# Half of the up product's k-tiles by seven block products, and the feed-forward in three parts

## The chip, the cores and the metric

The kernel runs on one NeuronCore of a Trainium2 chip. The metric is the device time of one execution in microseconds (us). Three runs of the kernel before took 1993.22, 1993.96 and 1994.38 us; their median, 1993.96 us, is the time before.

## The reference, cut to what matters

The reference is one layer of an encoder block on 256 tokens of width 2048: gated token mixers, cross-attention to 256 memory tokens, and a feed-forward. The change touches the feed-forward alone, in float32 throughout:

```
def _swiglu(h, w_gu, w_down):
    g, u = jnp.split(h @ w_gu, 2, axis=-1)     # h: 256 x 2048, w_gu: 2048 x 11264
    return (jax.nn.silu(g) * u) @ w_down       # w_down: 5632 x 2048
...
x = x + _swiglu(_rms(x, norm_ffn[i]), w_gu[i], w_down[i])
```

The first half of `w_gu` is called gate, the second half up, and `w_down` down.

## The kernel before, in words

**A product.** The large products go through `gemm_i` (lines 124 to 161). One call makes 512 output columns for all 256 tokens. The inner width is cut into k-tiles of 128; the tokens into two halves of 128, each with an accumulator in PSUM of 512 columns (a bank). Float32 accuracy is had from two rounded parts of each operand: with h and l for the high and low part, a product of one k-tile and one half of the tokens is three matmuls, h by h, h by l and l by h (lines 150 to 152), each with 128 columns of activations loaded as the stationary operand and 512 columns of weights streaming past. So 16 k-tiles are 16 x 2 x 3 = 96 matmuls.

**The weights.** `load_w` brings four k-tiles (1 MB, 2048 columns) into one of two buffers named `raw`, on SyncE's queue (SP). `split_w` (lines 110 to 122) makes from two k-tiles, 1024 columns, the high part on ScalarE (ACT, line 120) and then the low part, weights less high part, on VectorE (DVE, line 121). Both go into a tile named `wsp`, of which there are four. ACT may write a `wsp` only when the last matmul on the split of four before is done.

**The feed-forward** (lines 1048 to 1075). The normalised input lies transposed in `x2T_h` and `x2T_l`, 16 k-tiles each. A loop of 11 rounds makes 512 columns a round: a gate product (16 k-tiles), evacuated by ACT with SiLU to two tiles `gt`; an up product (16 k-tiles), evacuated by DVE, which multiplies it by `gt`; and `to_operand`, eight transposes on TensorE (PE, line 859) and two splits into `hT_h` and `hT_l`. The transposes of a round stand among the matmuls of the next gate. After the 11 rounds, four down products run over all 44 k-tiles of `hT`, and DVE adds the residual `x1` and the sums go out. Ahead of the feed-forward stands the output product of the cross-attention (`w_xo`, line 1038), whose four blocks are added to `x1` and turned by `to_operand` into `x2T`.

**The order.** A scheduler lays down each engine's order when the program is built; on the chip each engine follows its own order and waits on semaphores. Loads and splits of weights have the highest priority there (`WPRI`), evacuations the second (`EPRI`).

## Time and profile before

| | |
|---|---|
| median of three runs | 1993.96 us |
| the profiled execution's own time | 1992.28 us |
| its span, first to last instruction | 1990.5 us |
| PE busy | 1979.3 us, 99% |
| DVE busy | 1248.9 us, 63% |
| ACT busy | 973.9 us, 49% |
| DMA | 377.78 MB, 190 GB/s mean |
| gate and up, 11 rounds | 1256 to 1745 us of the span |
| down, four products | 1745 us to the end |

The profile is of one execution. Busy times count instructions under way; matmuls overlap each other, so that one shows as 0.39 us where the next starts 0.227 us later. What a matmul costs in a dense stream is therefore read from starts, not from durations; the same holds, less strongly, for DVE. "Idle before" and its releaser tell whom an engine waited for.

### The profile page before, as it was taken

The page shows a single profiled execution, that of the slowest core. Times are in us where ns is not written, and L with a number is a line of the kernel's source. Part 1 is how long each engine was busy: PE and PEld are TensorE (multiplying, and loading weights), DVE is VectorE, ACT ScalarE, POOL GpSimd, SP SyncE. Part 2 cuts the span into 40 slices and gives each one's busy share as a digit, 9 for nine tenths or more (in the row PEclk, how much of TensorE's full clock was granted, in tenths as well). Part 3 has the DMA queues.
Part 4 walks back from the last instruction along what each step waited for, and adds up shares of the span by engine and source line. Part 5 has one row for each costly group of instructions (what it writes and reads, how often), then busy time and mean ns, then how long its engine had stood idle before and what let it go on. Part 6 is the DMA issues. An engine that isn't in the chain of part 4 may idle for free.

```text
span 1990.5 us, 25137 instructions
## 1 busy us (share of the span) xinstructions
PE 1979.3 (99%) x9880; PEld 1665.5 (84%) x9880; DVE 1248.9 (63%) x1804; ACT 973.9 (49%) x1332; POOL 79.4 (4%) x142
## 2 busy tenths in 40 slices
PE   9999999999999999999999999999999999999999
PEld 7998888887888888888888888888888888888887
DVE  8968886769987967655545655545544444444443
ACT  7555655555444354554544545444444444443332
POOL 1002202000000000011000100000000000000000
PEclk9999999999999999999999999999999999999999
DMA  8554455455555655765455444555555555555553
GB/s 315 187 175 159 136 190 202 161 197 179 183 189 187 204 189 210 276 212 190 169 193 187 148 149 169 190 190 190 190 190 191 190 190 190 191 190 201 201 202 136
DMA packets 60406, 377.78 MB, mean 190 GB/s; under 512 B 6912, under 2 KB 8064, under 8 KB 18816
## 3 DMA queue, kind: packets, MB, share of 16 engines
q1 hardware_dynamic: 56880, 367.42, 52.6%
q0 software_dynamic: 2112, 6.82, 1.5%
q10 hardware_dynamic: 1296, 1.95, 0.3%
q8 instruction: 77, 1.26, 0.2%
q14 instruction: 41, 0.34, 0.0%
HBM read 374.06 MB, written 2.10 MB: 189 GB/s over the span
## 4 chain that ended last, share of the span: by engine, by line
PE 94%; DVE 2%; DMA 1%; ACT 1%; issue 1%; POOL 1%; SPq 0%; DVEq 0%; ACTq 0%; POOLq 0%
PE acc L151 28%; PE acc L150 28%; PE acc L152 28%; PE acc L175 2%; PE acc L176 2%; PE acc L177 2%; PE sm L859 1%; DMA raw<-in_w_in_dram 1%; DVE wsp L121 1%; PE sm L419 1%; PE sm L1028 1%; PE sm L1002 1%; ACT wsp L120 0%; PE sm L943 0%; PE sm L223 0%
## 5 line engine op out<-in xcount | busy, mean ns | idle before, releaser
L121 DVE TENSOR_TENSOR wsp<-raw,wsp 128x1024 fp32r<-128x1024 f32 (+2 forms) x700 | 833.2, 1193 | 648.1 <-ACT wsp L120 645.3
L120 ACT CAST wsp<-raw 128x1024 fp32r<-128x1024 f32 (+2 forms) x700 | 715.3, 1029 | 862.2 <-PE acc L152 638.9
L150 PE MATMUL acc<-wsp,x2T_h 128*128 128x512 f32 x704 | 274.9, 391 | 0.0
L151 PE MATMUL acc<-wsp,x2T_h 128*128 128x512 f32 x704 | 274.9, 391 | 0.0
L152 PE MATMUL acc<-wsp,x2T_l 128*128 128x512 f32 x704 | 273.9, 389 | 0.0
L151 PE MATMUL acc<-wsp,xT_h 128*128 128x512 f32 (+2 forms) x704 | 262.6, 374 | 1.3 <-DVE wsp L121 1.2
L152 PE MATMUL acc<-wsp,xT_l 128*128 128x512 f32 (+2 forms) x704 | 260.8, 371 | 0.0
L150 PE MATMUL acc<-wsp,xT_h 128*128 128x512 f32 (+2 forms) x704 | 260.1, 373 | 0.3 <-ACT wsp L120 0.3
L151 PEld LDWEIGHTS acc<-wsp,xT_h 128*128 128x128 f32 x704 | 132.2, 188 | 27.1 <-DVE wsp L121 3.4
L152 PEld LDWEIGHTS acc<-wsp,x2T_l 128*128 128x128 f32 x704 | 132.2, 188 | 27.1
L150 PEld LDWEIGHTS acc<-wsp,x2T_h 128*128 128x128 f32 x704 | 132.2, 188 | 27.1
L151 PEld LDWEIGHTS acc<-wsp,x2T_h 128*128 128x128 f32 x704 | 132.2, 188 | 27.0
L150 PEld LDWEIGHTS acc<-wsp,xT_h 128*128 128x128 f32 x704 | 132.0, 188 | 24.4 <-issue 1.3
L152 PEld LDWEIGHTS acc<-wsp,xT_l 128*128 128x128 f32 x704 | 132.3, 188 | 23.1 <-issue 0.3
L150 PE MATMUL acc<-wsp,hT_h 128*128 128x512 f32 x352 | 137.0, 389 | 0.0
L151 PE MATMUL acc<-wsp,hT_h 128*128 128x512 f32 x352 | 137.0, 389 | 0.0
L152 PE MATMUL acc<-wsp,hT_l 128*128 128x512 f32 x352 | 136.9, 389 | 0.0
L152 PE MATMUL acc<-wsp,eT_l 128*128 128x512 f32 x256 | 100.1, 391 | 0.0
L151 PE MATMUL acc<-wsp,eT_h 128*128 128x512 f32 x256 | 100.0, 390 | 0.0
L150 PE MATMUL acc<-wsp,eT_h 128*128 128x512 f32 x256 | 99.8, 390 | 0.0
L175 PE MATMUL acc<-xT_h,wsp 128*128 128x256 f32 x352 | 99.3, 282 | 0.0
L176 PE MATMUL acc<-xT_l,wsp 128*128 128x256 f32 x352 | 99.2, 282 | 0.0
(376 smaller groups left out, 2828.3 us busy)
## 6 DMA issues: line engine op xcount, KB each, us to landing
raw<-in_w_gu_dram SPq DMA_DIRECT2D x88, 1024.0 KB, 4.7
raw<-in_w_in_dram SPq DMA_DIRECT2D x68, 1024.0 KB, 4.9
raw<-in_w_down_dram SPq DMA_DIRECT2D x44, 1024.0 KB, 4.7
raw<-in_w_xkv_dram SPq DMA_DIRECT2D x32, 1024.0 KB, 4.7
raw<-in_w_ii_dram SPq DMA_DIRECT2D x22, 1024.0 KB, 4.9
raw<-in_w_out_dram SPq DMA_DIRECT2D x16, 1024.0 KB, 5.3
raw<-in_w_xq_dram SPq DMA_DIRECT2D x16, 1024.0 KB, 4.7
raw<-in_w_xo_dram SPq DMA_DIRECT2D x16, 1024.0 KB, 4.7
```

Of the source, the lines that this page charges most:

```text
L120: S.copy(hi[:, :n], raw[:, c0:c1])
L121: V.tensor_tensor(lo[:, :n], raw[:, c0:c1], hi[:, :n].bitcast(F32), ALU.subtract)
L150: PE.matmul(o, sh, h, start=(kt == 0), stop=False)
L151: PE.matmul(o, sh, lw, start=False, stop=False)
L152: mm = PE.matmul(o, xl[:, kt, t * P:(t + 1) * P], h, start=False, stop=(kt == nk - 1))
L175: PE.matmul(po, h, xh[:, kt, :], start=(kt == 0), stop=False)
L176: PE.matmul(po, h, xl[:, kt, :], start=False, stop=False)
L177: mm = PE.matmul(po, lo[:, j * P:(j + 1) * P], xh[:, kt, :], start=False, stop=(kt == nk - 1))
L419: PE.matmul(pb[e][:, i * T:(i + 1) * T], bT[q:q + 32, i, c, :], u[q:q + 32, c, :], start=True, stop=True, tile_position=(q, 0))
L859: PE.transpose(px[:, j * T + t * P:j * T + (t + 1) * P], srcs[t][:, (kp + j) * P:(kp + j + 1) * P], ident)
L1002: PE.matmul(pS[:, t * T:(t + 1) * T], qx[:, qi, d, t * P:(t + 1) * P], kx[:, ki, d], start=(d + i == 0), stop=(d == 3 and i == 2))
L1028: PE.matmul(po[:, j * T:(j + 1) * T], vx[:, vi, m, c0:c0 + P], pT[pi][:, m * T:(m + 1) * T], start=(m + i == 0), stop=(m == 1 and i == 2))
```

## The change

**Seven products for eight.** In the up product, k-tiles 0 to 7 stay as they were. K-tiles 8 to 15 are taken as four pairs of k-tiles (2, "q"), two halves of the tokens and two halves of the 512 columns ("h"): a 2 x 2 block product. Strassen's scheme in Winograd's form makes it from seven products of blocks where the plain form has eight. A product is now four pairs by three matmuls, each 128 columns stationary and 256 streaming (lines 232 to 234). Three of the seven run on in half banks of the two accumulators, on top of what k-tiles 0 to 7 left there; four go to banks of their own.

**Sums of the activations.** `pairs_operand` makes, for the blocks of k-tiles 8 to 15, the four sums and differences S1 to S4 beside the blocks themselves, and splits all eight; they lie in the upper half of `x2T_h` and `x2T_l` and in new tiles `x2S_h` and `x2S_l`. It replaces `to_operand` for two of the four blocks of `w_xo`.

**Sums of the weights.** `seven_weights` loads the last 8 k-tiles of an up (two loads of 1 MB) into a tile `sraw`, of which there is one, in the middle of the gate's loads, and makes four sums of 1024 columns on DVE (lines 192 to 195), one in place in `sraw` and three in a tile `ts`, of which there is one. Each of the seven weight blocks is then split as before (lines 224 and 225), 1024 columns at a time.

**Sums of the products.** ACT copies two of the products from PSUM to tiles `u` (line 240); DVE makes eight additions of 256 columns (line 251), six of which write to PSUM in place.

**Three parts.** The 11 rounds are cut into 4, 4 and 3. After each part, the four down products run over that part's 16, 16 or 12 k-tiles; the first two parts add to `x1` in place, the third adds and writes out. `hT` is a tile for one part.

The diff, cut to its core:

```diff
-    def gemm_i(xh, xl, nk, src, off, n, evac, first=None, e=0):
+    def gemm_i(xh, xl, nk, src, off, n, evac, first=None, e=0, then=None):
...
                 raw = load_w(blk, kk * n)
+                if k == 4 and then is not None:
+                    then()
...
+    def seven_weights(src, off):
+        raw = spool[0].tile([P, NS * 512], F32, tag="sraw", name=nm("sraw"))
+        off += P * (KD - NS) * 512
+        for i in range(2):
+            load_w(src[off:off + P * 2048].rearrange("(p f) -> p f", p=P), 2048,
+                   raw[:, i * 2048:(i + 1) * 2048])
+            off += P * 2048
+        ts = spool[0].tile([P, 3, 4, 256], F32, tag="ts", name=nm("ts"))
+        b11, b12, b21, b22 = blocks(raw)
+        t1, t2, t4 = (ts[:, i] for i in range(3))
+        V.tensor_tensor(t1, b11, b12, ALU.add)
+        V.tensor_tensor(b12, b12, b22, ALU.add)
+        V.tensor_tensor(t2, t1, b22, ALU.add)
+        V.tensor_tensor(t4, t2, b21, ALU.add)
+        return raw, ts
...
+    def gemm_s(xh, xl, sop, src, off, evac, weights):
...
+        def parts(b):
+            t = wp.tile([P, 2112], F32R, tag="wsp", name=nm("wsp"), bufs=4)
+            hi, lo = (t[:, 1024 * i + 48:1024 * i + 1072].rearrange("p (i c) -> p i c", c=256)
+                      for i in range(2))
+            with tc.high_priority(offset=WPRI):
+                S.copy(hi, b)
+                V.tensor_tensor(lo, b, hi.bitcast(F32), ALU.subtract)
+            return hi, lo
+
+        def product(o, i, b, start, stop):
+            hi, lo = parts(b)
+            for p in range(4):
+                sh, sl = sop(0, p, i), sop(1, p, i)
+                PE.matmul(o, sh, hi[:, p], start=start and p == 0, stop=False)
+                PE.matmul(o, sh, lo[:, p], start=False, stop=False)
+                PE.matmul(o, sl, hi[:, p], start=False, stop=stop and p == 3)
+            return o
...
+        product(c(0, 0), A12, b21, False, False)
+        product(c(0, 1), S4, b22, False, True)
+        u1 = kept(side(A11, b11))
+        v(c(0, 0), c(0, 0), u1, ALU.add)
+        u5 = kept(side(S1, t1))
+        p6 = side(S2, t2)
+        v(u1, p6, u1, ALU.add)
+        v(c(0, 1), c(0, 1), u5, ALU.add)
+        v(c(0, 1), c(0, 1), u1, ALU.subtract)
+        evac(0, pp[0])
+        product(c(1, 0), A22, t4, False, True)
+        p7 = side(S3, t3)
+        v(c(1, 1), c(1, 1), u5, ALU.add)
+        v(u1, p7, u1, ALU.add)
+        v(c(1, 0), c(1, 0), u1, ALU.add)
+        v(c(1, 1), c(1, 1), u1, ALU.subtract)
+        evac(1, pp[1])
...
+            V.tensor_tensor(b[:, S1], b[:, A21], b[:, A22], ALU.subtract)
+            V.tensor_tensor(b[:, S3], b[:, A11], b[:, A21], ALU.subtract)
+            V.tensor_tensor(b[:, S2], b[:, S1], b[:, A11], ALU.subtract)
+            V.tensor_tensor(b[:, S4], b[:, S2], b[:, A12], ALU.add)
...
-    hTh = p3.tile([P, KF, T], F32R, name="hT_h")
+    for c0, c1 in FF_PARTS:
+        nk = 4 * (c1 - c0)
+        hTh = p3.tile([P, nk, T], F32R, tag="hh", name=nm("hT_h"))
...
-        off = gemm_i(gTh, gTl, KD, a["w_gu"], off, 512, evg)
-        off = gemm_i(gTh, gTl, KD, a["w_gu"], off, 512, evu)
-        to_operand(sg, hTh, hTl, 4 * n)
+            def then(up=up, o=off + CH):
+                up["w"] = seven_weights(a["w_gu"], o)
+            off = gemm_i(mixed(0), mixed(1), KD, a["w_gu"], off, 512, evg, then=then)
+            off = gemm_s(gT[0], gT[1], sop, a["w_gu"], off, evu, up["w"])
+            to_operand(sg, hTh, hTl, 4 * (n - c0))
...
+                    if not last:
+                        d = x1[:, t, n * 512:(n + 1) * 512]
+                        V.tensor_tensor(d, po, d, ALU.add)
+                        return
```

**PE, from k-tile 13 on in the up of the second round.** `acc` is an accumulator, `wsp` a split of the weights, `x2T` and `x2S` the activations and their sums. Before:

```order
L150 MATMUL acc_11223<-wsp_11322,x2T_h 128x512
L151 MATMUL acc_11223<-wsp_11322,x2T_h 128x512
L152 MATMUL acc_11223<-wsp_11322,x2T_l 128x512
L150 MATMUL acc_11222<-wsp_11337,x2T_h 128x512 [waits Activation_49]
L151 MATMUL acc_11222<-wsp_11337,x2T_h 128x512 [waits DVE_49]
L152 MATMUL acc_11222<-wsp_11337,x2T_l 128x512
```

Now, where the whole k-tiles end and the first of the seven products begins:

```order
L211 MATMUL acc_11321<-wsp_11371,x2T_h 128x512
L212 MATMUL acc_11321<-wsp_11371,x2T_h 128x512
L213 MATMUL acc_11321<-wsp_11371,x2T_l 128x512
L232 MATMUL acc_11320<-wsp_11386,x2T_h 128x256 [waits Activation_49]
L233 MATMUL acc_11320<-wsp_11386,x2T_h 128x256 [waits DVE_49]
L234 MATMUL acc_11320<-wsp_11386,x2T_l 128x256
```

The matmuls of k-tiles 8 to 15 now have 256 columns instead of 512; there are 84 of them a round for the 48 of before, and a new split is taken up every 12, as before.

**DVE, from the end of an up to the next gate.** `wsp<-raw` is a low part, `gt<-acc` the evacuation of the up, `hT_l` the low part of the next operand. Before:

```order
L121 TENSOR_TENSOR wsp_11322<-raw_11320,wsp_11322 128x1024 [waits DMAHW5_49,Activation_49]
L121 TENSOR_TENSOR wsp_11337<-raw_11320,wsp_11337 128x1024 [waits Activation_49]
L121 TENSOR_TENSOR wsp_11374<-raw_11372,wsp_11374 128x1024 [waits DMAHW6_49,Activation_49]
L121 TENSOR_TENSOR wsp_11389<-raw_11372,wsp_11389 128x1024 [waits Activation_49]
L121 TENSOR_TENSOR wsp_11406<-raw_11404,wsp_11406 128x1024 [waits DMAHW7_49,Activation_49]
L1060 SCALAR_TENSOR_TENSOR gt_11088<-acc_11222,rst,gt_11088 128x512 [waits PE_49]
L1060 SCALAR_TENSOR_TENSOR gt_11089<-acc_11223,rst,gt_11089 128x512 [waits PE_49]
L121 TENSOR_TENSOR wsp_11421<-raw_11404,wsp_11421 128x1024 [waits Activation_49]
L121 TENSOR_TENSOR wsp_11438<-raw_11436,wsp_11438 128x1024 [waits DMAHW0_49,Activation_49]
L215 TENSOR_TENSOR hT_l<-sm_11354,hT_h 128x512 [waits Activation_49]
L215 TENSOR_TENSOR hT_l<-sm_11361,hT_h 128x512 [waits Activation_49]
```

Now, from the last two of the seven low parts on; `u` are the copies that ACT made, `sm` a product in a bank of its own:

```order
L225 TENSOR_TENSOR wsp_11473<-ts_11219,wsp_11473 128x1024 [waits Activation_49]
L225 TENSOR_TENSOR wsp_11489<-sraw_11216,wsp_11489 128x1024 [waits Activation_49]
L251 TENSOR_TENSOR acc_11320<-acc_11320,u_11432 128x256 [waits Activation_49]
L121 TENSOR_TENSOR wsp_11529<-raw_11527,wsp_11529 128x1024 [waits DMAHW6_49,Activation_49]
L251 TENSOR_TENSOR u_11432<-sm_11453,u_11432 128x256 [waits DVE_49,PE_49]
L251 TENSOR_TENSOR acc_11320<-acc_11320,u_11451 128x256 [waits Activation_49]
L121 TENSOR_TENSOR wsp_11544<-raw_11527,wsp_11544 128x1024 [waits Activation_49]
L251 TENSOR_TENSOR acc_11321<-acc_11321,u_11451 128x256 [waits PE_49]
L251 TENSOR_TENSOR acc_11320<-acc_11320,u_11432 128x256 [waits DVE_49]
L121 TENSOR_TENSOR wsp_11569<-raw_11559,wsp_11569 128x1024 [waits DMAHW7_49,Activation_49]
L121 TENSOR_TENSOR wsp_11584<-raw_11559,wsp_11584 128x1024 [waits Activation_49]
```

and, following on without a gap, through the weight sums (`ts`, `sraw`) of the next round to the gate's sixth split:

```order
L1214 SCALAR_TENSOR_TENSOR gt_11178<-acc_11320,rst,gt_11178 128x512 [waits DVE_49]
L251 TENSOR_TENSOR u_11432<-sm_11488,u_11432 128x256
L192 TENSOR_TENSOR ts_11564<-sraw_11561 128x1024 [waits DMAHW1_49,DMAHW0_49]
L251 TENSOR_TENSOR acc_11321<-acc_11321,u_11432 128x256 [waits DVE_49]
L193 TENSOR_TENSOR sraw_11561<-sraw_11561 128x4x256 [waits DVE_49]
L194 TENSOR_TENSOR ts_11564<-ts_11564,sraw_11561 128x1024
L251 TENSOR_TENSOR acc_11321<-acc_11321,u_11432 128x256 [waits DVE_49]
L195 TENSOR_TENSOR ts_11564<-ts_11564,sraw_11561 128x1024 [waits DVE_49]
L121 TENSOR_TENSOR wsp_11601<-raw_11599,wsp_11601 128x1024 [waits DMAHW2_49,Activation_49]
L1214 SCALAR_TENSOR_TENSOR gt_11179<-acc_11321,rst,gt_11179 128x512 [waits DVE_49]
L121 TENSOR_TENSOR wsp_11616<-raw_11599,wsp_11616 128x1024 [waits Activation_49]
```

Between the last split of the up and the fifth of the next gate there now stand eight additions and four weight sums. The first sum waits for the loads of `sraw`, and every later low part stands behind it in DVE's order.

**SP's queue, loads of weights at the start of the third round's gate.** Before:

```order
L102 DMA raw_11288<-in_w_gu_dram 128x2048 [waits DMAHW2_49,DVE_49]
L102 DMA raw_11320<-in_w_gu_dram 128x2048 [waits DMAHW3_49,DVE_49]
L102 DMA raw_11372<-in_w_gu_dram 128x2048 [waits DMAHW4_49,DVE_49]
L102 DMA raw_11404<-in_w_gu_dram 128x2048 [waits DMAHW5_49,DVE_49]
L102 DMA raw_11436<-in_w_gu_dram 128x2048 [waits DMAHW6_49,DVE_49]
```

Now:

```order
L102 DMA raw_11322<-in_w_gu_dram 128x2048 [waits DMAHW2_49,DVE_49]
L102 DMA raw_11354<-in_w_gu_dram 128x2048 [waits DMAHW3_49,DVE_49]
L102 DMA raw_11527<-in_w_gu_dram 128x2048 [waits DMAHW4_49,DVE_49]
L102 DMA raw_11559<-in_w_gu_dram 128x2048 [waits DMAHW5_49,DVE_49]
L102 DMA sraw_11561<-in_w_gu_dram 128x2048 [waits DMAHW1_49,DMAHW0_49,DVE_49]
L102 DMA sraw_11561<-in_w_gu_dram 128x2048
```

The two loads of `sraw` stand ahead of the gate's third and fourth load. The first of them waits for DVE, which must have read the last block of the `sraw` before.

## Rows read from the trace of the kernel before

**Rows 1.** The page: busy time of PE with its share and instructions, and the span in 40 equal slices, in tenths, for PE, DVE and PE's granted clock.

```profile
PE 1979.3 (99%) x9880; PEld 1665.5 (84%) x9880; DVE 1248.9 (63%) x1804; ACT 973.9 (49%) x1332; POOL 79.4 (4%) x142
PE   9999999999999999999999999999999999999999
DVE  8968886769987967655545655545544444444443
PEclk9999999999999999999999999999999999999999
```

**Rows 2.** Who PE waited for, over the whole span: us in total, times, longest.

```profile
PE sm L223 <- ACT ev L663: 2.8, 1, 2.8
PE acc L237 <- DVE ev L234: 1.5, 1, 1.5
PE acc L151 <- DVE wsp L121: 1.2, 2, 1.0
PE sm L631 <- ACT t2k L624: 0.7, 2, 0.4
PE acc L150 <- ACT wsp L120: 0.3, 1, 0.3
PE sm L562 <- DVE g_az L559: 0.2, 1, 0.2
```

**Rows 3.** Busy time of each engine in three stretches: the second round of gate and up, all 11 rounds, and a stretch of the mixers in which DVE is nearly full. Columns: length, busy us (instructions) of PE, PE's loads, DVE, ACT, POOL, granted clock, DMA share, GB/s.

```profile
1306.79:1351.24 44.45, 44.45 (x203) 36.84 (x201) 22.21 (x20) 19.11 (x20) 0.00 (x0) 1.00 0.54 190
1256.00:1745.00 489.00, 489.00 (x2203) 405.49 (x2202) 245.01 (x225) 213.35 (x227) 1.46 (x4) 1.00 0.54 190
640.00:700.00 60.00, 60.00 (x279) 48.51 (x278) 54.19 (x85) 25.28 (x29) 2.15 (x4) 1.00 0.59 198
```

**Rows 4.** PE's timeline in the first gate, matmuls of 512 columns: start, duration, line. The first and the last of 40 in a dense stream.

```profile
1264.70 0.39 PE L150 MATMUL acc<-wsp,x2T_h 128*128 128x512 f32 x1
...
1273.54 0.39 PE L150 MATMUL acc<-wsp,x2T_h 128*128 128x512 f32 x1
```

**Rows 5.** PE's timeline around the product with `w_glu`, which follows on a stream of 512 columns: 108 matmuls of 256 columns from 734.15 on, then 512 again.

```profile
733.92 0.39 PE L152 MATMUL acc<-wsp,xT_l 128*128 128x512 f32 x1
734.15 0.28 PE L175 MATMUL acc<-yg,wsp 128*128 128x256 f32 x1
...
746.87 0.39 PE L150 MATMUL acc<-wsp,ys 128*128 128x512 f32 x1
```

**Rows 6.** PE's timeline in the 256-column blocks of `w_in`, where, as in the change, the weights stream and activations are stationary: the first and the last of 52 matmuls.

```profile
139.06 0.28 PE L150 MATMUL acc<-wsp,xT_h 128*128 128x256 f32 x1
...
145.07 0.28 PE L150 MATMUL acc<-wsp,xT_h 128*128 128x256 f32 x1
```

**Rows 7.** PE's timeline in a product of `w_ii` (256 columns of activations stream): the first and the last of 56 matmuls.

```profile
254.75 0.28 PE L175 MATMUL acc<-xT_h,wsp 128*128 128x256 f32 x1
...
260.98 0.28 PE L176 MATMUL acc<-xT_l,wsp 128*128 128x256 f32 x1
```

**Rows 8.** Groups of instructions of DVE, shapes kept apart: line, operation, out<-in, count, busy us, mean ns, idle before. `acc` and `sm` lie in PSUM.

```profile
L121 DVE TENSOR_TENSOR wsp<-raw,wsp 128x1024 fp32r<-128x1024 f32 x658 | 802.5, 1222 | 625.7 <-ACT wsp L120 623.1
L450 DVE TENSOR_TENSOR_SCAN s2k<-s5p,xx 128x256 f32<-128x256 f32 x48 | 30.9, 675 | 0.0
L1060 DVE SCALAR_TENSOR_TENSOR gt<-acc,rst,gt 128x512 f32<-128x512 f32 x22 | 15.4, 743 | 0.0
L385 DVE TENSOR_TENSOR E<-s2k 128x256 f32<-128x256 f32 x24 | 10.0, 416 | 0.2
L830 DVE TENSOR_TENSOR part<-acc,gt 128x512 f32<-128x512 f32 x8 | 5.4, 680 | 0.0
L833 DVE TENSOR_TENSOR part<-part,gt 128x512 f32<-128x512 f32 x8 | 5.3, 681 | 0.0
L215 DVE TENSOR_TENSOR ya<-sm,ya 128x256 fp32r<-128x256 f32 x8 | 3.4, 419 | 0.6 <-ACT ya L214 0.6
```

**Rows 9.** DVE's timeline where it works without a gap: start, duration. The last row needs the result of the one before it.

```profile
501.98 1.22 DVE L121 TENSOR_TENSOR wsp<-raw,wsp 128x1024 fp32r<-128x1024 f32 x1
503.12 0.42 DVE L383 TENSOR_TENSOR s2k<-ea,eb 128x256 f32<-128x256 f32 x1
503.45 0.42 DVE L384 TENSOR_TENSOR s2k<-ea,eb 128x256 f32<-128x256 f32 x1
503.79 1.22 DVE L121 TENSOR_TENSOR wsp<-raw,wsp 128x1024 fp32r<-128x1024 f32 x1
504.92 0.42 DVE L385 TENSOR_TENSOR E<-s2k 128x256 f32<-128x256 f32 x1
505.37 0.69 DVE L443 TENSOR_TENSOR s2k<-xx,E 128x512 f32<-128x512 f32 x1
```

**Rows 10.** The high parts on ACT, as one group: line, out<-in, count, busy us, mean ns, idle before and who ended it.

```profile
L120 ACT CAST wsp<-raw 128x1024 fp32r<-128x1024 f32 x658 | 688.6, 1053 | 831.9 <-PE acc L152 632.1 <-DMA raw<-in_w_in_dram 76.0 <-DMA raw<-in_w_out_dram 22.0
```

**Rows 11.** Loads: the page's row for `w_gu` (count, KB each, median us from issue to landing), and the DMA engines' busy share (tenths) and GB/s in 40 slices of 703 to 712 us, where two loads of 1 MB run one behind the other.

```profile
raw<-in_w_gu_dram SPq DMA_DIRECT2D x88, 1024.0 KB, 4.7
...
DMA  0000099905778999989895997997999200000000
GB/s 0 0 0 0 0 255 182 182 0 146 255 328 364 400 437 473 400 364 473 364 510 219 400 473 328 437 510 328 437 473 473 109 0 0 0 0 0 0 0 0
```

More of the change, by code (lines that the diff above doesn't have):

```diff
@@ L148, in gemm_i @@
                         lw = lo[:, j * n:(j + 1) * n]
-                        sh = xh[:, kt, t * P:(t + 1) * P]
+                        sh = half(xh, kt, t)
                         PE.matmul(o, sh, h, start=(kt == 0), stop=False)
                         PE.matmul(o, sh, lw, start=False, stop=False)
-                        mm = PE.matmul(o, xl[:, kt, t * P:(t + 1) * P], h, start=False,
+                        mm = PE.matmul(o, half(xl, kt, t), h, start=False,
                                        stop=(kt == nk - 1))
@@ L161, in gemm_i, with blocks @@
         return off
+    NS = 8
+    A11, A12, A21, A22, S1, S3, S2, S4 = range(8)
+    spool = [None]
+    def blocks(x):
+        rv = x.rearrange("p (i q h c) -> p q h i c", q=2, h=2, c=256)
+        return [rv[:, q, h] for q in range(2) for h in range(2)]
+    def seven_weights(src, off):
[13 more added lines that the diff above has]
+        return raw, ts
@@ new lines, in gemm_s, with kept, c, side @@
+    def gemm_s(xh, xl, sop, src, off, evac, weights):
+        pp = [acc(), acc()]
+        n = 512
+        for k in range(0, KD - NS, 4):
+            raw = load_w(src[off:off + P * 4 * n].rearrange("(p f) -> p f", p=P), 4 * n)
+            off += P * 4 * n
+            for k2 in range(0, 4, 2):
+                hi, lo = split_w(raw, k2 * n, (k2 + 2) * n)
+                for t in range(2):
+                    for j in range(2):
+                        kt = k + k2 + j
+                        h, lw = hi[:, j * n:(j + 1) * n], lo[:, j * n:(j + 1) * n]
+                        PE.matmul(pp[t], half(xh, kt, t), h, start=(kt == 0), stop=False)
+                        PE.matmul(pp[t], half(xh, kt, t), lw, start=False, stop=False)
+                        PE.matmul(pp[t], half(xl, kt, t), h, start=False, stop=False)
+        raw, ts = weights
+        b11, t3, b21, b22 = blocks(raw)
+        t1, t2, t4 = (ts[:, i] for i in range(3))
+        def parts(b):
[14 more added lines that the diff above has]
+            return o
+        def kept(o):
+            u = spool[0].tile([P, 256], F32, tag="u", name=nm("u"), bufs=4)
+            with tc.high_priority(offset=EPRI):
+                S.copy(u, o)
+            return u
+        def c(t, h):
+            return pp[t][:, h * 256:(h + 1) * 256]
+        def side(i, w):
+            return product(sm()[:, :256], i, w, True, True)
+        def v(dst, x, y, op):
+            with tc.high_priority(offset=EPRI):
+                V.tensor_tensor(dst, x, y, op)
+        product(c(0, 0), A12, b21, False, False)
[15 more added lines that the diff above has]
+        evac(1, pp[1])
+        return off + P * NS * n
@@ L1049, in tile_block @@
[L1049 removed]
+    spool[0] = p3
     off = 0
[L1051 to L1063 removed]
@@ L1064, in tile_block, with evg, evu, ev @@
-    off = 0
-    for n in range(4):
-        def ev(t, po, n=n):
-            o = t2k()
-            with tc.high_priority(offset=EPRI):
-                for c in range(0, 512, 256 if n == 3 else 512):
-                    d = slice(c, c + (256 if n == 3 else 512))
-                    g = slice(n * 512 + d.start, n * 512 + d.stop)
-                    V.tensor_tensor(o[:, d], po[:, d], x1[:, t, g], ALU.add)
-                    (nc.sync if c else nc.scalar).dma_start(out[t * P:(t + 1) * P, g], o[:, d])
-        off = gemm_i(hTh, hTl, KF, a["w_down"], off, 512, ev)
+    for c0, c1 in FF_PARTS:
+        nk = 4 * (c1 - c0)
+        hTh = p3.tile([P, nk, T], F32R, tag="hh", name=nm("hT_h"))
+        hTl = p3.tile([P, nk, T], F32R, tag="hl", name=nm("hT_l"))
+        for n in range(c0, c1):
+            sg = [t2k("gt", 2), t2k("gt", 2)]
+            up = {}
+            def evg(t, po, sg=sg):
+                with tc.high_priority(offset=EPRI):
+                    S.activation(sg[t], po, AF.Silu, scale=rst[:, 6 + t:7 + t])
+            def evu(t, po, sg=sg):
+                with tc.high_priority(offset=EPRI):
+                    V.scalar_tensor_tensor(sg[t], po, rst[:, 6 + t:7 + t], sg[t], ALU.mult,
+                                           ALU.mult)
+            def then(up=up, o=off + CH):
[3 more added lines that the diff above has]
+            to_operand(sg, hTh, hTl, 4 * (n - c0))
+        for n in range(4):
+            def ev(t, po, n=n, last=(c1 == FF // 512)):
+                with tc.high_priority(offset=EPRI):
+                    if not last:
+                        d = x1[:, t, n * 512:(n + 1) * 512]
+                        V.tensor_tensor(d, po, d, ALU.add)
+                        return
+                    o = t2k()
+                    for c in range(0, 512, 256 if n == 3 else 512):
+                        d = slice(c, c + (256 if n == 3 else 512))
+                        g = slice(n * 512 + d.start, n * 512 + d.stop)
+                        V.tensor_tensor(o[:, d], po[:, d], x1[:, t, g], ALU.add)
+                        (nc.sync if c else nc.scalar).dma_start(out[t * P:(t + 1) * P, g],
+                                                                o[:, d])
+            gemm_i(hTh, hTl, nk, a["w_down"], (n * FF + c0 * 512) * 512, 512, ev)
@@ L1075, in tile_block @@
     p3.release()
+    pS.release()
     px1.release()
```

54 lines of the change are left out of this document (39 added, 15 removed).

## The prediction

> **What bounds the kernel now.** [...] Next, who PE waited for: 6.7 us in the whole span [rows 2]. Then the feed-forward by stretches: a round of gate and up is 44.45 us with DVE half full and ACT at 43%, and over all 11 rounds PE is busy for the whole 489.00 us, so that none of the waiting lies there [rows 3]. So the end moves if, and as far as, PE's own stream in the 11 rounds gets shorter, and as long as no other engine makes PE wait. The last thing to read is what a matmul costs there. Its row says 0.39 us, but that is latency; the price is the distance between starts, from 1264.70 to 1273.54 over 39 matmuls, 226.7 ns for 512 columns [rows 4]. 192 of them are 43.52 us, which leaves 0.93 us of a round for its eight transposes, 0.12 us each [rows 3, 4].
>
> **PE's stream, the term that is meant to shrink.** A round loses the 48 matmuls of k-tiles 8 to 15: 48 x 226.7 ns = 10.88 us. It gains 84 of 256 columns. Such matmuls occur in two speeds. After a stream of 512 columns, 108 of them ran from 734.15 to 746.87, 117.8 ns each [rows 5]; with weights streaming over stationary activations, as here, 51 took 6.01 us, 117.8 ns [rows 6]; but in a product of another kind 55 took 6.23 us, 113.3 ns, exactly half of the wide ones [rows 7]. I take 117.8, from the rows nearest in what precedes and in what streams: 84 x 117.8 = 9.90 us. A round is 0.98 us shorter, 11 rounds 10.8 us. At 113.3 it would be 9.52, 1.36 and 15.0 us: the other end. New splits are taken up every 12 matmuls as before, and inside rows 6 a split changed after every 12 as well, at no cost beside the 117.8.
>
> [...]
>
> Down loses and adds no matmul: 44 k-tiles are 16 + 16 + 12. The transposes stay eight a round.
>
> **What is hidden beside PE, and by how much.** ACT makes seven high parts a round for the four of before, 3 x 1.05 us more [rows 10], and two copies: it was busy 19.1 of 44.45 us [rows 3], so there is room. DVE gets three more low parts (1.14 us each when nothing holds it: the next instruction starts 1.14 us after a low part of 1.22), four weight sums of 1024 columns (the same kind and width, 1.14), eight additions of 256 (0.335 apart) [rows 8, 9]: 3.4 + 4.6 + 2.7 = 10.7 us on top of 22.2 [rows 3], 33 of 43.5 us. In the mixers DVE was busy 54 of 60 us with PE at 60 of 60 [rows 3], so fullness as such does not stop PE. What can is DVE's order: between the up's last low part and the gate's fifth stand eight additions, four weight sums and an evacuation, and the first sum waits for the loads of `sraw`.
>
> I follow that chain once. Zero is when the third of the seven products ends, which frees the `wsp` for the seventh block. ACT makes its high part to 1.05, DVE its low part from 1.08 to 2.30 [rows 8, 10], free for the next at 2.22. Up to the first weight sum stand six additions, four low parts and one evacuation (0.67): 6 x 0.335 + 4 x 1.14 + 0.67 = 7.24, so DVE is there at 9.46 [rows 8, 9]. With the seventh low part `sraw` is free and its two loads go out at 2.3. One lands 4.7 us after its issue; two behind each other took 27 slices of 0.225 us for 2.1 MB, so I allow 3.0 for the second: 10.0 [rows 11]. The first sum therefore starts at 10.0, not 9.46. Four sums and two additions, 5.23 us, lead to 15.2, and the gate's fifth low part is done at 16.5. PE: the fourth product starts at -0.16 (a matmul ends 0.28 after its start, the next comes 0.12 after it), four products end at 5.49 [rows 5], four splits of 12 wide matmuls at 16.37 [rows 4], two transposes bring 16.6, and the fifth low part is wanted two matmuls later, at 17.06. It is there 0.5 us early. All later low parts come 1.2 us apart and are wanted 2.7 us apart. So no stall, but a thin cover: it is gone if the chain is half a microsecond late, and from then on each further microsecond costs one in about ten rounds.
>
> Two prices of the chain are in no row. DVE writes PSUM in place in six additions; rows show it only reading there, and reading costs nothing (680 ns with `acc`, 681 without; 419 with `sm`, 416 without [rows 8]). I take 0.42 us as lower end and as value, and two passes, 0.84 us, as the upper end. Weight blocks are read in four runs of 256 with a step; rows show 1024 in one run; I take that price. [...]
>
> **The rest, off the path.** The operand sums during `w_xo` (four differences of 128 columns and a split of 1024 for each pair) are wanted from the gate's k-tile 12 on, 12 x 6 x 0.227 = 16 us after its start; their 5 us of DVE lie beside that. In the first gate the `sraw` loads wait for the last matmul of `w_xo` and hold up the gate's fourth load in SP's queue: three loads, 4.7 + 3 + 3 = 10.7 us after the gate's start [rows 11], wanted 16.3 us after it. The 16 additions to `x1` at the ends of the first two parts (0.68 each) fall in down, where nothing waits for them; four accumulators let PE go on. At each start of a down the last round's `hT` is wanted 12 k-tiles in. The tail after the last matmul is the same. I cost all this at nothing; its cover is named.
>
> **Sum.** Profiled time 1992.28 (span 1990.5 and 1.8 around it) less 10.8 is 1981.5; the median of the runs lies 1.7 above the profiled one, so 1993.96 - 10.8 = 1983.1 us.
>
> **Rivals.**
> - *Half the width at half the spacing.* If the products run at 113.3 ns [rows 7], 15.0 us are saved: 1979.0. For it: that speed holds for many products in a row once it is met. Against: the three kinds of stretch that resemble this one show 117.8. [...]
> - *The chain eats part of it.* If the second load of `sraw` lands 1 us later, or the chain is otherwise 1 us longer, PE stands 0.5 us in each of ten rounds: 5 us back, 1988. If the two loads took 4.7 us each, the sum starts at 11.7 and PE stands 1.2: 12 us back, 1995, no change. For it: the cover is 0.5 us and the load is the step that binds. Against: the DMA engines move over 400 GB/s when two loads meet [rows 11].
> - *DVE's writes to PSUM are slow, and the kernel gets slower.* Each addition that takes d longer than 0.42 makes the chain 8 d longer: from 9.46 + 5.23 + 1.22 = 15.9 against 17.06 a loss starts at d = 0.14, eats the gain of 0.98 at d = 0.27, and at two passes, d = 0.42, PE stands 2.2 us a round: 22 - 10.8 = 11 us slower, 2005. For it: no row shows such a write. Against: reading PSUM costs DVE nothing extra.
>
> **How the numbers follow.** Forecast (1981.5 to 1985.5) 0.53; half the spacing 0.15; part of it eaten (1985.5 to 1990) 0.15; all of it eaten, within 0.2% (1990 to 1998) 0.09; slower 0.08. 0.2%, 4 us, is about what a measurement of this kernel tells from no change. Faster by more: 0.53 + 0.15 + 0.15 = 0.83. The range of 8 in 10 takes in both spacings and nearly all of the partly eaten case, 1978.5 to 1989.5, and leaves out the last two cases.
>
> **What would show it.** Right: a round between like rows 43.5 us apart; 84 matmuls of 256 columns with starts 117.8 ns apart; PE waiting for nothing in the rounds; DVE busy some 33 us a round; the sums of line 192 starting as the load lands. Wrong: PE idle at line 157 on DVE at the gate's fifth split, released by the low part that follows the weight sums (the chain), with line 192 held by DMA (the loads) or line 251 longer than 0.42 us (PSUM); or starts 113 ns apart. A gain in the rounds that the down parts take back would show as PE waits on lines 156 to 158 with `hT`, and would refute the section on the rest.

## The result and the profile after

| | changed | before, beside it | ratio, 95% interval |
|---|---|---|---|
| median (4 runs each) | 1984.36 us (1983.69 to 1985.4) | 1994.17 us (1993.22 to 1995.83) | 0.995 (0.9933 to 0.9968) |
| again, later (5 and 9 runs) | 1985.08 us | 1993.84 us | 0.9952 (0.994 to 0.9965) |
| profiled execution | 1983.69 us, span 1981.9 | 1992.28 us, span 1990.5 | |

9.8 us faster, at 1984.4 us where 1983.1 was forecast; both intervals leave out 1. The first lines of the page, as in [rows 1]:

```profile
PE 1970.5 (99%) x10276; PEld 1676.0 (85%) x10276; DVE 1376.1 (69%) x1997; ACT 1015.9 (51%) x1391; POOL 79.3 (4%) x142
PE   9999999999999999999999999999999999999999
DVE  8968886769987957655544665677765677756764
PEclk9999999999999999999999999999999999999999
```

PE has 396 matmuls more and is busy 8.8 us less; DVE rises by 127 us, all in the last third, and the clock stays full. The same windows as in [rows 3], two rounds one behind the other:

```profile
1353.50:1397.00 43.50, 43.18 (x235) 37.17 (x234) 33.25 (x38) 22.07 (x26) 0.00 (x0) 1.00 0.51 193
1397.05:1440.55 43.50, 43.50 (x238) 37.73 (x237) 32.31 (x37) 23.90 (x27) 0.00 (x0) 1.00 0.51 194
```

A round is 43.5 us (44.45 in [rows 3]), DVE is busy 32 to 33 us of it, and the first of the two holds 0.32 us of idle PE. The products, first and last of the 84 matmuls of a round in PE's timeline:

```profile
1334.80 0.28 PE L232 MATMUL acc<-wsp,x2T_h 128*128 128x256 f32 x1
...
1344.58 0.28 PE L234 MATMUL sm<-wsp,x2S_l 128*128 128x256 f32 x1
```

83 steps in 9.78 us are 117.8 ns each, the speed of [rows 5, 6]. In other rounds it is the same. The new operations on DVE, by shape, with the line, the operation, count, busy us and mean ns:

```profile
L225 DVE TENSOR_TENSOR wsp<-sraw,wsp 128x1024 fp32r<-128x1024 f32 x44 | 53.8, 1225 | 51.8 <-ACT wsp L224 51.8
L251 DVE TENSOR_TENSOR acc<-acc,u 128x256 f32<-128x256 f32 x66 | 27.0, 425 | 0.1
L192 DVE TENSOR_TENSOR ts<-sraw 128x1024 f32<-128x1024 f32 x11 | 13.5, 1225 | 4.7 <-DMA sraw<-in_w_gu_dram 4.2
```

Adding in place in PSUM takes 425 ns (416 without PSUM [rows 8]), and a low part from a strided block takes 1225 ns (1222 from one run). L192 shows where the chain waits: for a load.

**The account of the 9.2 us.** A length that runs of one kernel repeat better than their total is the feed-forward itself, from the start of its first matmul with `x2T` to the start of the last matmul of all. Before it is 1256.98 to 1985.74, 728.77 us; after 1257.62 to 1977.15, 719.53 us, and 719.52 in the second profiled run. The difference is 9.24, where the distances between starts alone (11 x (48 x 226.67 - 84 x 117.78) ns) give 10.85. So 1.6 us came back. About 1.0 of it lies in two places, each at the fifth split behind a run of the seven products. The first is in a gate (PE's timeline, then DVE's in the same round):

```profile
1355.84 0.61 PE L156 MATMUL acc<-wsp,x2T_h 128*128 128x512 f32 x2
1356.78 0.50 PE L157 MATMUL acc<-wsp,x2T_h 128*128 128x512 f32 x1 [0.32 <-DVE wsp L121]
```

```profile
1348.32 0.42 DVE L251 TENSOR_TENSOR u<-sm,u 128x256 f32<-128x256 f32 x1
1350.29 1.23 DVE L192 TENSOR_TENSOR ts<-sraw 128x1024 f32<-128x1024 f32 x1 [1.55 <-DMA sraw<-in_w_gu_dram]
...
1354.37 1.22 DVE L195 TENSOR_TENSOR ts<-ts,sraw 128x1024 f32<-128x1024 f32 x1
1355.50 1.22 DVE L121 TENSOR_TENSOR wsp<-raw,wsp 128x1024 fp32r<-128x1024 f32 x1
```

Two matmuls of 226.7 ns from 1355.84 lead to 1356.30; the next came at 1356.78, when the fifth low part (1355.50 + 1.22) was there: 0.48 us late, and the following start another 0.11. The second place is not in a gate. After the second part's last up the down comes, and there the fifth split is one of `w_down`; the weight sums of the next part stand ahead of its low part, although their products come a whole down later:

```profile
1704.34 0.61 PE L156 MATMUL acc<-wsp,hT_h 128*128 128x512 f32 x2
1705.10 0.50 PE L157 MATMUL acc<-wsp,hT_h 128*128 128x512 f32 x1
```

Here the start at 1705.10 is 0.30 us late and the next 0.11. In both places the first weight sum had waited for the second load of `sraw`, 1.55 and 1.38 us. In an ordinary round it waits little:

```profile
1392.42 0.41 DVE L251 TENSOR_TENSOR u<-sm,u 128x256 f32<-128x256 f32 x1
1392.90 1.23 DVE L192 TENSOR_TENSOR ts<-sraw 128x1024 f32<-128x1024 f32 x1
...
1398.11 1.22 DVE L121 TENSOR_TENSOR wsp<-raw,wsp 128x1024 fp32r<-128x1024 f32 x1
```

The forecast's chain can be laid on these rows. Zero is the end of the third product, 0.16 us after the fourth starts; the fourth starts at 1383.14 in the ordinary round and at 1339.04 in the late one:

| us after zero | forecast | ordinary round | late round |
|---|---|---|---|
| loads of `sraw` issued | 2.3 | 2.4 | 2.4 |
| first lands | 7.0 | 7.0 | 7.1 |
| second lands | 10.0 | 9.5 | 11.0 |
| first weight sum starts | 10.0 | 9.6 | 11.1 |
| fifth low part done | 16.5 | 16.0 | 17.5 |
| wanted by PE | 17.06 | 17.1 | 17.1 |

So the cover is 1.06 us in an ordinary round, and a load that lands 1.5 us later uses it up. The view of the line that issues the loads gives, for the late round and then the ordinary one, the time to landing of the two loads (the first is the min, the second the max):

```profile
  DVE ts L192: 1.6, 1
...
DMA to landing us min/median/max: 4.7/6.5/8.2
```

```profile
DMA to landing us min/median/max: 4.6/5.7/6.8
```

A third second load was late too (landed at 1306.11, 10.5 us after that round's zero); its fifth low part came just in time, and PE lost 0.11 us there. What is left, 0.5 us, is not spread evenly: it lies in the two dozen 512-column matmuls that follow a group of transposes. There 110 steps are some 230 to 240 ns, 0.71 us in all above 226.67, where the kernel before has 31 such steps and 0.17 us. No run shows why.

### The profile page after: what moved, and what is told of

Read it like the earlier page. It is cut to its first block, busy times and chain, and to the rows that moved or that the text cites. A ratio compares the mean times of both kernels' runs of the same rounds, so it can differ in the third digit from the quotient of the medians.

```text
span 1981.9 us, 26213 instructions
## 1 busy us (share of the span) xinstructions
PE 1970.5 (99%) x10276; PEld 1676.0 (85%) x10276; DVE 1376.1 (69%) x1997; ACT 1015.9 (51%) x1391; POOL 79.3 (4%) x142
## 3 DMA queue, kind: packets, MB, share of 16 engines
q8 instruction: 80, 1.31, 0.3%
## 4 chain that ended last, share of the span: by engine, by line
PE 93%; DVE 3%; DMA 2%; ACT 1%; issue 1%; POOL 1%; SPq 0%; DVEq 0%; ACTq 0%; POOLq 0%
PE acc L157 24%; PE acc L158 23%; PE acc L156 23%; PE acc L283 2%; PE acc L285 2%; PE acc L284 2%; PE acc L212 2%; PE acc L211 2%; PE acc L213 2%; PE sm L232 1%; PE sm L967 1%; PE sm L234 1%; PE sm L233 1%; DMA sraw<-in_w_gu_dram 1%; DVE wsp L121 1%
## 5 line engine op out<-in xcount | busy, mean ns | idle before, releaser
L121 DVE TENSOR_TENSOR wsp<-raw,wsp 128x1024 fp32r<-128x1024 f32 (+2 forms) x656 | 775.7, 1190 | 440.3 <-ACT wsp L120 436.1
L120 ACT CAST wsp<-raw 128x1024 fp32r<-128x1024 f32 (+2 forms) x656 | 666.0, 1026 | 728.4 <-PE acc L158 401.6
L157 PE MATMUL acc<-wsp,x2T_h 128*128 128x512 f32 x264 | 103.9, 394 | 0.3 <-DVE wsp L121 0.3
L158 PE MATMUL acc<-wsp,x2T_l 128*128 128x512 f32 x264 | 103.5, 392 | 0.0
L283 PE MATMUL acc<-xT_h,wsp 128*128 128x256 f32 x352 | 99.5, 283 | 0.0
L285 PE MATMUL acc<-xT_h,wsp 128*128 128x256 f32 x352 | 98.6, 281 | 0.0
L156 PE MATMUL acc<-wsp,x2T_h 128*128 128x512 f32 x264 | 96.5, 390 | 0.0
L225 DVE TENSOR_TENSOR wsp<-sraw,wsp 128x1024 fp32r<-128x1024 f32 x44 | 53.8, 1225 | 51.8 <-ACT wsp L224 51.8
L157 PEld LDWEIGHTS acc<-wsp,hT_h 128*128 128x128 f32 x352 | 66.1, 188 | 14.3 <-DVE wsp L121 0.6
```

The costliest lines, as they stand in the source:

```text
L120: S.copy(hi[:, :n], raw[:, c0:c1])
L121: V.tensor_tensor(lo[:, :n], raw[:, c0:c1], hi[:, :n].bitcast(F32), ALU.subtract)
L156: PE.matmul(o, sh, h, start=(kt == 0), stop=False)
L157: PE.matmul(o, sh, lw, start=False, stop=False)
L158: mm = PE.matmul(o, half(xl, kt, t), h, start=False, stop=(kt == nk - 1))
L225: V.tensor_tensor(lo, b, hi.bitcast(F32), ALU.subtract)
```

## The experiments

Each ran beside the kernel before on its chip. "Feed-forward" is the length defined above, in the profiled run; since two runs of the changed kernel gave 719.53 and 719.52, and two kernels with the same matmuls 728.77 both, it tells tenths of a microsecond apart that the medians can't.

| run | median us | before us | ratio, 95% interval | feed-forward us |
|---|---|---|---|---|
| e1_parts | 1993.63 | 1993.59 | 1.0001 (0.9992 to 1.001) | 728.77 |
| e2_gpsimd_sums | 1992.48 | 1993.59 | 0.9994 (0.9985 to 1.0003) | 729.11 |
| e3_sums_behind | 1983.68 | 1993.59 | 0.9951 (0.9938 to 0.9965) | 718.44 |
| e4_two_more | 2010.58 | 1993.59 | 1.0085 (1.0072 to 1.0099) | 745.73 |
| e5_offset16 | 1984.47 | 1992.91 | 0.9954 (0.9942 to 0.9967) | 720.03 |
| e6_offset0 | 1985.43 | 1992.91 | 0.9959 (0.9946 to 0.9971) | 721.57 |
| e7_nine_less | 1974.36 | 1992.91 | 0.9904 (0.9889 to 0.9919) | 710.31 |
| e8_eighth | 2001.33 | 1992.91 | 1.0039 (1.0027 to 1.0052) | 736.19 |
| e9_less_behind | 1973.15 | 1993.84 | 0.9895 (0.988 to 0.9911) | 706.64 |
| e10_twelve | 2014.43 | 1993.84 | 1.0102 (1.0088 to 1.0116) | 751.09 |
| e11_changed_again | 1985.08 | 1993.84 | 0.9952 (0.994 to 0.9965) | 719.52 |
| e12_offset32 | 1987.24 | 1994.44 | 0.9962 (0.9949 to 0.9974) | 721.83 |

**The parts alone.** The kernel before with `FF_PARTS` and the partial downs, and nothing else.

> The kernel before with the feed-forward in three parts (4, 4 and 3 column blocks of gate and up, each part followed by a partial down that adds into x1), and nothing else of the change. Theory: the parts cost nothing, because every matmul stays and the eight added PSUM evacuations (745 ns each) lie beside matmuls: 1994.2 us, within 0.3. Rival: the 1.6 us by which the feed-forward of the changed kernel fell short of its 10.85 us of saved TensorE time are lost at the part boundaries: 1995.8 us.

The same time and the same feed-forward to 0.01 us: parts, additions to `x1` and boundaries cost nothing. The rival falls. (The additions to `x1` are 16, of 0.68 us each, where the expectation says eight of 745 ns.)

**An eighth product, and nine matmuls fewer.** `product` gets a count `n` of pairs; the second product takes 8 (its four pairs twice) in e8_eighth, as below, and 1 in e7_nine_less.

```diff
-        product(c(0, 1), S4, b22, False, True)
+        product(c(0, 1), S4, b22, False, True, 8)
```

> The changed kernel with an eighth product's matmuls put back, and no more: the second product's 12 matmuls of 256 columns are issued twice from the same blocks (its part of the sum is counted twice in the output). Theory (each matmul costs its spacing, nothing else on the path changes): 12 x 117.78 ns x 11 = 15.5 us more than the changed kernel, 1999.9 us, which is 5.7 us slower than the kernel before: the saving is the missing product alone, and the half-width matmuls cost 0.45 us a round of it. Rival (the gain comes from another place, such as the moved low parts): 1984 to 1990 us.

> The changed kernel with the second product (the right half of the first 128 rows' tile) made from one of its four pairs of k-tiles only, so 9 of 84 matmuls of 256 columns a round are left out; copies, low parts, sums and additions stay. That part of the sum is left out of the output. Theory (TensorE sets the time, the rest lies beside it): 9 x 117.78 ns x 11 = 11.7 us less than the changed kernel, 1972.7 us, with rather more stall at the fifth low part, since the chain of 9 to 17 us starts after these matmuls and does not shrink. Rival (VectorE's rows are at their limit in a round of 43.5 us): less than half of it, 1979 us or more.

The eighth product costs 16.66 us in the feed-forward, of which 132 x 117.78 ns = 15.55 are its matmuls; the other 1.1 is more stall, at four fifth splits in place of two (2.2 us, by starts, for 1.0). With it the change is a loss. The saved product is thus the whole gain, and nothing else of the change gives any. With nine fewer, 9.22 us of the 11.66 show. The rest is stall at the gate's fifth split, four times instead of two and longer (PE's waits in the feed-forward):

```profile
PE acc L157 <- DVE wsp L121: 2.6, 4, 0.8
```

**The sums out of the way of the fifth low part.** `seven_weights` returns its four sums as a function, called in the gate once its sixth low part is issued; `low[0]` is that low part.

```diff
+                if (k, k2) == (8, 2) and then is not None:
+                    sums()
...
+        def sums():
+            with tc.issue_after(low[0]):
+                V.tensor_tensor(t1, b11, b12, ALU.add)
```

> The changed kernel with the loads where they are, and the four weight sums held behind the sixth low part of gate on VectorE in place of standing ahead of the fifth. Theory (chain of the second sraw load): the sums wait for nothing any more and the low parts run on, 1.0 to 1.4 us less than the changed kernel, 1983.1 us. Rival (spacing and transposes): 1984.4 us.

> Both edits in one: nine of the 84 matmuls of a round left out (that part of the sum is left out of the output), and the four weight sums held behind the sixth low part of gate. With the nine left out alone the time was 1974.4 us, 10.0 us under the changed kernel where 11.7 us of TensorE were taken away. Theory (what is missing is stall in the chain of the second sraw load): it comes back, 1983.7 - 11.7 = 1972.0 us, with no wait at the fifth low part left. Rival (VectorE's 33 us of work are the limit of the shorter round): 1974.4 us or more.

DVE's timeline at the place of the late round: the fifth and sixth low parts wait for nobody but ACT, and the first sum follows them, with no DMA named.

```profile
1349.75 0.75 DVE L1221 SCALAR_TENSOR_TENSOR gt<-acc,rst,gt 128x512 f32<-128x512 f32 x1
1353.77 2.36 DVE L122 TENSOR_TENSOR wsp<-raw,wsp 128x1024 fp32r<-128x1024 f32 x2 [3.27 <-ACT wsp L121]
1356.05 1.22 DVE L199 TENSOR_TENSOR ts<-sraw 128x1024 f32<-128x1024 f32 x1
```

Both stalls are gone, though in this run too two second loads landed late (1350.09 and 1698.36): the feed-forward is 1.09 us shorter, 718.44. The medians can't tell 0.7 us (the ratios' intervals lie over each other, as do those of e7_nine_less and e9_less_behind), so this and the next comparison are read from the traces alone. With the nine matmuls left out as well, the feed-forward falls by 11.80 us against e3_sums_behind (forecast 11.66) and by 3.67 against e7_nine_less, and PE waits for nothing in it. VectorE's 33 us a round are not the limit; its order is.

**The chain made longer.** The last sum three times, and every split of the gate from the fifth on held behind the last of them.

```diff
         V.tensor_tensor(t4, t2, b21, ALU.add)
-        return raw, ts
+        V.tensor_tensor(t4, t2, b21, ALU.add)
+        end = V.tensor_tensor(t4, t2, b21, ALU.add)
+        return raw, ts, end.ins
...
+                if k >= 8 and then is not None:
+                    with tc.issue_after(last[0]):
+                        hi, lo = split_w(raw, k2 * n, (k2 + step) * n, e)
```

> The changed kernel with two more sums (the last sum repeated, 1.22 us each) a round, and the fifth low part of gate held behind the sums: the chain is 2.43 us longer, VectorE works 2.4 us more in a round of 43.5. Theory (the chain has some 0.5 to 0.9 us of cover): 1.5 to 1.9 us of stall in each of 8 to 11 rounds, 12 to 21 us, so 1996 to 2005 us, in the stall at the matmuls that read the fifth low part. Rival (VectorE's work is hidden beside the matmuls as a whole, 10 us of each round being free): 1984.4 us.

More than expected: 26.2 us in the feed-forward. PE and DVE in an ordinary round, PE in the first gate, and two windows with the clock (columns as in [rows 3], granted clock third from the end):

```profile
1416.00 0.82 PE L974 MATMUL sm<-cc,gt 128*128 128x128 f32 x6
1418.17 0.50 PE L162 MATMUL acc<-wsp,x2T_h 128*128 128x512 f32 x1 [1.35 <-DVE wsp L122]
```

```profile
1408.63 1.23 DVE L197 TENSOR_TENSOR ts<-sraw 128x1024 f32<-128x1024 f32 x1 [0.19 <-DMA sraw<-in_w_gu_dram]
...
1413.84 0.74 DVE L1221 SCALAR_TENSOR_TENSOR gt<-acc,rst,gt 128x512 f32<-128x512 f32 x1
1414.50 1.21 DVE L201 TENSOR_TENSOR ts<-ts,sraw 128x1024 f32<-128x1024 f32 x1
1415.75 1.23 DVE L202 TENSOR_TENSOR ts<-ts,sraw 128x1024 f32<-128x1024 f32 x1
1416.89 4.62 DVE L122 TENSOR_TENSOR wsp<-raw,wsp 128x1024 fp32r<-128x1024 f32 x4
```

```profile
1276.17 0.80 PE L162 MATMUL acc<-wsp,x2T_h 128*128 128x512 f32 x1 [5.22 <-DVE wsp L122]
1276.77 0.63 PE L163 MATMUL acc<-wsp,x2T_l 128*128 128x512 f32 x1
1277.20 0.63 PE L161 MATMUL acc<-wsp,x2T_h 128*128 128x512 f32 x1
```

```profile
1260.00:1270.00 10.00, 10.00 (x50) 8.33 (x49) 6.32 (x11) 6.56 (x12) 1.47 (x4) 1.00 0.74 308
1276.80:1279.50 2.70, 2.70 (x8) 2.13 (x7) 2.70 (x4) 0.00 (x0) 0.00 (x0) 0.50 0.41 94
```

An ordinary round stalls for 1.6 us, but the edit moved more than the two sums. The second evacuation of the up (L1221), which stood behind the fifth low part, now stands ahead of it: from the start of the first sum to the end of the fifth low part it is 9.48 us where it was 6.43, 3.05 longer. On PE six transposes (L974) moved ahead of the matmul that wants this low part, so that it is wanted 0.56 us later. 3.05 less 0.56 and less the cover of 1.06 leaves 1.4, near the 1.6 seen, so the cover read above is borne out. The stall comes in nine of the eleven rounds; behind the first two parts the fifth split is a down's, which this edit does not hold.

What the expectation lacked is the clock. After gaps of 5.6, 2.1 and 2.9 us between starts, in the first three rounds, it fell to 0.50, and 21 steps between matmuls were 427 ns in place of 227, 4.2 us together. After the later gaps, of 1.6 us, it did not fall.

**The sums on GpSimd.** The four lines begin with `G.` in place of `V.`.

> The changed kernel with its four weight sums a round issued on GpSimd in place of VectorE. Theory (the give-back sits in the chain second sraw load, four sums, fifth low part of gate): without the sums in VectorE's row no round waits, 1.0 to 1.4 us less than the changed kernel, 1983.1 us. Rival: the give-back is matmul spacing and transposes, not this chain: 1984.4 us, as the changed kernel. A third case, that GpSimd's 44 sums slow VectorE's low parts or come too late for their products: slower, by at least the 0.5 us of cover that a round had, so over 1990 us.

The third case. DVE's timeline, and GpSimd's in the same microseconds:

```profile
1361.42 9.12 DVE L121 TENSOR_TENSOR wsp<-raw,wsp 128x1024 fp32r<-128x1024 f32 x3 [3.44 <-ACT wsp L120]
1370.46 1.28 DVE L323 TENSOR_TENSOR hT_l<-sm,hT_h 128x512 fp32r<-128x512 f32 x2
```

```profile
1360.36 2.40 POOL L193 TENSOR_TENSOR sraw<-sraw 128x1024 f32<-128x1024 f32 x1
1362.72 3.39 POOL L194 TENSOR_TENSOR ts<-ts,sraw 128x1024 f32<-128x1024 f32 x1
1366.19 3.27 POOL L195 TENSOR_TENSOR ts<-ts,sraw 128x1024 f32<-128x1024 f32 x1
```

Three low parts of 1.22 us take 9.12 while the sums run, and they end at 1363.84, 1367.19 and 1370.53, each 1.08 us after a sum has ended; over the feed-forward L121 has a mean of 1468 ns for 1221. So in these rows one low part is done behind each sum; what makes the two engines take turns was not shown.

Most of the 9.6 us that the feed-forward lost, 6.0, lies in the first gate. There VectorE still makes the sums of the activations; beside GpSimd's sums three of them took 1.9 to 2.5 us in place of 0.29, PE waited 3.09 us, and 12 slow steps followed, the first matmul at 0.80 us, as the one ahead of the steps at 0.50 in e4_two_more:

```profile
1279.62 0.80 PE L157 MATMUL acc<-wsp,x2S_h 128*128 128x512 f32 x1 [3.09 <-DVE wsp L121]
```

**The place of the split blocks.** 16, 0 and 32 elements into the tile for 48, in `parts`.

```diff
-            hi, lo = (t[:, 1024 * i + 48:1024 * i + 1072].rearrange("p (i c) -> p i c", c=256)
+            hi, lo = (t[:, 1024 * i + 16:1024 * i + 1040].rearrange("p (i c) -> p i c", c=256)
```

> The changed kernel with the split weight blocks of the products written 16 elements into their tile in place of 48, and nothing else. Before, the 256-column matmuls of the first projections with x moving came 113.3 ns apart from blocks at 16 elements and those with weights moving 117.8 ns; the products' came 117.78 ns apart. If the offset of the moving block sets this: 924 x 4.45 ns = 4.1 us less than the changed kernel, 1980.3 us. If not: 1984.4 us.

> The same with the blocks at the tile's start (0 elements). If the offset of the moving block sets the spacing, the products' matmuls move off 117.78 ns, towards 113.3 ns (1980.3 us) or beyond it the other way, by the same 4 us (1988.5 us); if not: 1984.4 us.

> The changed kernel with the products' split blocks 32 elements into their tile. At 16 and at 48 elements their matmuls came 117.6 to 118.4 ns apart, at 0 elements 120.0 ns. If a multiple of 32 is what matters, 120 ns again and about 1986.4 us; if 0 alone is bad, 117.8 ns and 1984.4 us; if 32 is the good place, 113.3 ns and 1980.3 us.

At 16 the spacing stays 117.8 ns. At 0 nearly every step is 120 (first and last of 84, below: 9.95 us over 83 steps); at 32 the steps alternate between 118, 120 and 122, with the same mean. Both add 2.0 to 2.3 us to the feed-forward:

```profile
1335.14 0.28 PE L232 MATMUL acc<-wsp,x2T_h 128*128 128x256 f32 x1
...
1345.09 0.28 PE L234 MATMUL sm<-wsp,x2S_l 128*128 128x256 f32 x1
```

No place gave the 113.3 ns of [rows 7]. That speed did come up in other runs, though, in the same kind of product from blocks at 48 elements. In the first up of e10_twelve (the next run), PE waited in the middle of the products:

```profile
1286.57 0.28 PE L241 MATMUL acc<-wsp,x2T_h 128*128 128x256 f32 x1
...
1288.92 0.28 PE L240 MATMUL acc<-wsp,x2S_h 128*128 128x256 f32 x1
1289.64 0.39 PE L241 MATMUL acc<-wsp,x2S_h 128*128 128x256 f32 x1 [0.44 <-DVE wsp L232]
...
1291.65 0.28 PE L240 MATMUL sm<-wsp,x2T_h 128*128 128x256 f32 x1
...
1299.92 0.28 PE L241 MATMUL sm<-wsp,x2T_h 128*128 128x256 f32 x1
```

Ahead of the wait 20 steps took 117.8 ns each; from 1291.65 on, 73 steps took 113.3 each. In its second up, with no such wait, they ran at 117.8. In e7_nine_less the last 11 of the 75 matmuls, which stand behind two strays of 512 columns, settled at 113.3 too. So the speed goes with what came just before in PE's stream, and not with the kind of product; what exactly sets it, and whether it can be had for all 84, was not tried.

**Twelve k-tiles by seven products**, on e3_sums_behind, as an attempt at a faster version: `NS = 12`, products in two halves of three pairs, six parts.

> The version with the sums held behind, and 12 of 16 k-tiles of up by seven products instead of 8 (each product's blocks split in two halves of three pairs; the feed-forward in six parts, to find room for the larger weight sums). TensorE: 24 x 226.67 = 5.44 us of 512-column matmuls a round go, 42 x 117.78 = 4.95 us come, 0.49 us less a round, 5.4 us in all, so 1978.3 us if VectorE keeps up. VectorE: 2 low parts go (2.45 us), 14 of 768 columns stand for 7 of 1024 (from 1.225 us for 1024, some 0.92 us each: 12.9 for 8.6 us), sums 1.5 times as long (7.3 for 4.9 us): 37.5 us of 43. Rival: in the products themselves VectorE has 12.9 us of low parts and 4.9 us of additions and evacuations beside 14.8 us of matmuls; if its lead of three blocks doesn't cover the 3 us, up to 3 us of stall a round, 1984 to 2011 us.

Slower than the kernel before and than e3_sums_behind, and not for the rival's reason. The spacings alone give the 5.4 us. But in the second round's gate DVE was idle for 5.70 us, behind ACT, which stood 9.75 us:

```profile
1312.65 1.07 ACT L330 CAST hT_h<-sm 128x512 fp32r<-128x512 f32 x2 [9.75 <-PE sm L975]
1313.61 3.90 ACT L121 CAST wsp<-raw 128x1024 fp32r<-128x1024 f32 x4
```

The built order had put the copies of the transposes ahead of the gate's fifth high part on ACT; PE came to these transposes after four splits and then had no fifth: gaps of 2.0 and then 0.9 us between starts in five such rounds (1312.70, 1448.29 and so on), with the clock below 1.00 behind three of them (0.50 from 1316.10 to 1319.00; 0.74 as the mean of 1451.00 to 1454.00 and 0.81 of 1720.60 to 1723.00). And six parts mean six starts of a down. Five of them want their last `hT` after 4 k-tiles: 0.9 us of stall there and 0.7 at the fifth split. The last part has one round only and wants its `hT` at once: over 5 us. These gaps, the starts and the slow steps make some 32 of the 38 us to account for (32.7 more than e3_sums_behind, and 5.4 not gained); the rest is open. Whether 12 k-tiles pay in another order was not tried.

**The changed kernel again.**

> The changed kernel once more, on the chip and beside the runs of the two others, so that differences under 1 us can be read: 9.8 us under the kernel before, as the first time; the version with the sums held behind was 9.9 us under it on another chip.

8.8 us under before, as the first within the intervals; its two stalls are in the same two places (at 1356.70 and 1705.04).

## Why the prediction was right, and what was mis-sized

- *PE's term.* Right to the row: 117.78 ns and 226.67 ns, 10.85 us for the forecast 10.8. The other end, 113.3 ns, did not come in the changed kernel. One of the two grounds for the choice was luck. "What precedes" is borne out by the runs above. "What streams", and "a product of another kind" for [rows 7], are not: [rows 5] and [rows 7] are both of line 175, with activations streaming, at both speeds.
- *Hidden work.* Right: DVE 32 to 33 us a round for the forecast 33, beside full PE. The parts cost nothing, shown by e1_parts, and in the first gate PE waited for nothing. "I cost all this at nothing" fails at one place: PE stood 0.41 us on `hT` matmuls in the down behind the second part (1705.10). That is the sign which the prediction named against its section on the rest. It was not `hT` that came late there, but the fifth low part, behind the weight sums of the next part: the chain was followed into the gate alone, and at a part's end it runs into the down.
- *The two unknown prices of the chain.* Both at their lower end: 425 ns in PSUM (416 without), 1225 ns strided (1222 from one run). So the rival of slow writes has no ground.
- *The chain.* Its mechanism was right and its length within 0.5 us. What was mis-sized is "I allow 3.0 for the second" load: it is 2.5 us behind the first in most rounds and 3.3 to 3.9 in three. The rival "the chain eats part of it" is true in two places of eleven; it took 1.0 us, not 5. That it is the chain is shown from both sides: with the sums behind the sixth low part the stalls vanish, with two sums more nine rounds stall.
- *The 1.3 us* between 1983.1 and 1984.4. In the trace 1.6 us are missing: 1.0 in these two places, 0.1 in the third late round, 0.5 in the steps behind transposes, whose cause is open. The 0.3 between 1.6 and 1.3 is less than the medians can tell.

*Why these loads are late* was only read, not tried. The page of the profile has `q8 instruction: 80, 1.31`: 80 packets with 1.31 MB, 16 KB each, that the view calls instruction. In the changed kernel the second load was late in three rounds; in each of them one such packet ran between the first load's issue and the second's landing, here in a window of 2 us of the late round of above, and none did in the ordinary round of above (1386 to 1393):

```profile
q1 hardware_dynamic: 110, 0.78, 94.5%
q8 instruction: 1, 0.02, 2.9%
```

The same rounds were hit in both runs of the changed kernel, and others in e7_nine_less and e8_eighth, with other counts of matmuls.

The two traces of the changed kernel and those of the nine variants with the same loads (all runs but e1_parts and e10_twelve) have 121 such pairs of loads. From the first issue to the second landing a pair took 7.1 to 7.4 us, or 7.5 to 9.0 where it was late. In 41 pairs such a packet started between; 36 of these were late, and in the other five it started within the last 0.7 us. Of the 80 pairs without, five were late. No run moved a packet, and none shows what sets when one starts, so this is a strong coincidence and not shown as the cause.
